# RMSNorm over 16,384 rows on one core: the first store moved ahead of the second tile's load, a coarser first load, and the work split anew over three engines

## The chip, the core and the metric

The kernel runs on one core of a Trainium2 chip. The metric is the device time of one execution in microseconds (us). Before the change, eight runs gave a median of 162.51 us (162.01 to 163.07).

## The reference

The input `x` is 16 x 1024 x 512 in float32, that is 16,384 rows of 512 numbers, 33.55 MB; the output is as large. Each row is divided by its root mean square and multiplied by a vector `gamma` of 512 numbers:

```python
eps = 1e-5
rms = np.sqrt(np.mean(x ** 2, axis=-1, keepdims=True) + eps)
return (x / rms * gamma).astype(np.float32)
```

## The kernel before

**Tiles.** The rows are cut into four tiles. A tile puts R = 32 consecutive rows on each of the 128 partitions, so "a row" below always means one row on every partition: 128 x 512 float32, 262 KB. There are three buffers in on-chip memory (`slot0` to `slot2`), each of one tile; the fourth tile reuses `slot0`. The scaled result overwrites its input in the slot and is stored from there.

**Groups.** A tile is worked on in four groups of G = 8 rows. `row_stats` (from line 65) gives the reciprocal root mean squares of a group, `apply` (line 88) scales its rows, and `transfers` (line 102) asks for the loads and stores that belong after it. The loop at the end of the program takes the statistics of the next group ahead of scaling the present one.

**Engines.** In groups of even number ScalarE squares one row at a time and adds it up in the same operation (line 78; each is followed by a small read of the accumulator). In groups of odd number ScalarE squares four rows into PSUM (line 72) and VectorE adds them up (line 73). ScalarE takes the root (line 84), VectorE the reciprocal (line 85). VectorE alone scales: one operation per row multiplies it by its scalar and by `gamma_b`, a copy of gamma on all partitions (line 90). GpSimd does nothing but set constants. TensorE runs one matrix product, which spreads gamma over the partitions (line 57).

**Queues.** All large transfers are issued by SyncE, loads at line 42 and stores at line 45, in program order: an issue that waits for a semaphore holds every later one. SyncE issues, and the 16 DMA engines move the data. The order is: tile 0 in pieces of 8, 8 and 16 rows, the whole of tile 1, then row 0's store, half of tile 2's load, row 1's store, a quarter of tile 2's load, row 2's store, the last quarter, the rest of tile 0's stores, and so on. A store waits for the scaling of the rows that it takes. A load into `slot0` for tile 3 waits for tile 0's stores.

**Order on the engines.** Before the change, a scheduler chooses the order of each engine's instructions within what the dependences allow.

Of the kernel before, what the change touches and what calls it, by code (L numbers as in the profile page):

```python
# [1 line left out]

# [4 lines left out]


@with_exitstack
def kernel(  # L10
    ctx: ExitStack,
    tc: tile.TileContext,
    x: bass.AP,
    gamma: bass.AP,
    out: bass.AP,
):
    nc = tc.nc
    P = nc.NUM_PARTITIONS
    eps = 1e-5
    fp32 = mybir.dt.float32  # L20
    AF = mybir.ActivationFunctionType
    OP = mybir.AluOpType

    xf = x.flatten_outer_dims()
    of = out.flatten_outer_dims()
    N, D = xf.shape
    R = 32
    G = 8
    H = 4
    assert N == 4 * P * R  # L30

    xv = xf.rearrange("(t p r) d -> t p r d", p=P, r=R)
    ov = of.rearrange("(t p r) d -> t p r d", p=P, r=R)

    const = ctx.enter_context(tc.tile_pool(name="const", bufs=1))
    stats = ctx.enter_context(tc.tile_pool(name="stats", bufs=4))
    psum = ctx.enter_context(tc.tile_pool(name="psum", bufs=2, space=bass.MemoryType.PSUM))

    slots = [const.tile([P, R, D], fp32, name=f"slot{i}") for i in range(3)]

    def load(t, slot, r0, r1):
        nc.sync.dma_start(out=slots[slot][:, r0:r1], in_=xv[t][:, r0:r1])

    def store(t, slot, r0, r1):
        nc.sync.dma_start(out=ov[t][:, r0:r1], in_=slots[slot][:, r0:r1])

    load(0, 0, 0, 8)
    load(0, 0, 8, 16)
    load(0, 0, 16, 32)
    load(1, 1, 0, 32)  # L50

    gamma_row = const.tile([1, D], fp32)
    nc.scalar.dma_start(out=gamma_row, in_=gamma.unsqueeze(0))
    ones_col = const.tile([1, P], fp32)
    nc.vector.memset(ones_col, 1.0)  # L55
    gamma_psum = psum.tile([P, H, D], fp32, name="sq")
    nc.tensor.matmul(gamma_psum[:, 0], ones_col, gamma_row, start=True, stop=True)  # L57
    gamma_b = const.tile([P, D], fp32)
    nc.vector.tensor_copy(out=gamma_b, in_=gamma_psum[:, 0])  # L59

    eps_t = const.tile([P, 1], fp32)
    nc.vector.memset(eps_t, eps)  # L62
    sq_scratch = const.tile([P, D], fp32)

    def row_stats(slot, g):
        ss = stats.tile([P, G], fp32, name="ss")
        rms = stats.tile([P, G], fp32, name="rms")
        rstd = stats.tile([P, G], fp32, name="rstd")
        if (g // G) % 2:
            for h in range(0, G, H):  # L70
                sq = psum.tile([P, H, D], fp32, name="sq")
                nc.scalar.activation(out=sq, in_=slots[slot][:, g + h : g + h + H, :], func=AF.Square)  # L72
                nc.vector.tensor_reduce(  # L73
                    out=ss[:, h : h + H], in_=sq, axis=mybir.AxisListType.X, op=OP.add
                )
        else:
            for r in range(G):
                nc.scalar.activation(  # L78
                    out=sq_scratch,
                    in_=slots[slot][:, g + r, :],  # L80
                    func=AF.Square,
                    accum_out=ss[:, r : r + 1],
                )
        nc.scalar.activation(out=rms, in_=ss, func=AF.Sqrt, bias=eps_t, scale=1.0 / D)  # L84
        nc.vector.reciprocal(out=rstd, in_=rms)  # L85
        return rstd

    def apply(slot, g, rstd):
        for r in range(G):
            nc.vector.scalar_tensor_tensor(  # L90
                out=slots[slot][:, g + r, :],
                in0=slots[slot][:, g + r, :],
                scalar=rstd[:, r : r + 1],
                in1=gamma_b,
                op0=OP.mult,
                op1=OP.mult,
            )

    groups = [(t, g) for t in range(4) for g in range(0, R, G)]
    slot_of = [0, 1, 2, 0]  # L100

    def transfers(t, g):
        if (t, g) == (0, 0):
            store(0, 0, 0, 1)
            load(2, 2, 0, 16)
            store(0, 0, 1, 2)
            load(2, 2, 16, 24)
            store(0, 0, 2, 3)
            load(2, 2, 24, 32)
        elif (t, g) == (0, 24):  # L110
            store(0, 0, 3, 32)
        elif (t, g) == (1, 8):
            store(1, 1, 0, 16)
            load(3, 0, 0, 16)
            load(3, 0, 16, 32)
        elif (t, g) == (1, 24):
            store(1, 1, 16, 32)
        elif (t, g) == (2, 24):
            store(2, 2, 0, 32)
        elif (t, g) == (3, 8):  # L120
            store(3, 0, 0, 16)
        elif (t, g) == (3, 24):
            store(3, 0, 16, 32)

    ahead = row_stats(0, 0)
    for k, (t, g) in enumerate(groups):
        rstd = ahead
        if k + 1 < len(groups):
            tn, gn = groups[k + 1]
            ahead = row_stats(slot_of[tn], gn)  # L130
        apply(slot_of[t], g, rstd)
        transfers(t, g)


# [1 line left out]
_INS = ['x', 'gamma']  # L136
_OUTS = [((16, 1024, 512), 'float32')]


# [23 lines left out]
```

## Time and profile before

The profile is of one execution; the span is from its first to its last instruction on the core.

| | |
|---|---|
| median of 8 runs | 162.51 us |
| the profiled execution's own time | 162.31 us |
| its span | 160.5 us |
| VectorE busy | 122.6 us (76%) |
| ScalarE busy | 80.1 us (50%) |
| GpSimd busy | 0.2 us |
| bytes moved by DMA | 67.13 MB, mean 418 GB/s over the span |

"Busy" is the time in which an engine ran instructions. In a line of the groups of instructions, what follows the name of the operation is out<-in with partitions x elements; after the bar come the busy time in us and the mean duration of one instruction in ns, then the engine's idle time just before them and what ended it. Instructions on one engine overlap a little, so that the step from one start to the next can be shorter than a duration; the chain of waits gives start, length and number of a run of instructions, from which that step is seen.

### The profile page before, as it was taken

To read this page: it belongs to the slowest core of one execution; us is meant where nothing else is said; L and a number is where in the kernel's file an instruction comes from. 1 tells how busy PE (TensorE), PEld (TensorE's weight loads), DVE (VectorE), ACT (ScalarE), POOL (GpSimd) and SP (SyncE) were. 2 spreads that over 40 slices of the span, in tenths; PEclk is the share of its full clock that TensorE was granted. 3 is DMA by queue.
4 is the path that set the end of the run, shared out by engine and by line. 5 is a ranking of instruction groups with operands and counts; after the bars stand their busy time and mean duration, and the time that the engine had idled before them with its cause. 6 is when DMAs were issued, how large, how long until landed. Compare 5 with 4: busy or idle time off the path is not lost.

```text
span 160.5 us, 415 instructions
## 1 busy us (share of the span) xinstructions
PE 2.0 (1%) x2; PEld 0.5 (0%) x2; DVE 122.6 (76%) x163; ACT 80.1 (50%) x162; POOL 0.2 (0%) x4
## 2 busy tenths in 40 slices
PE   4000000000000000000000000000000000000000
PEld 1000000000000000000000000000000000000000
DVE  0102999999995099999999999999999999950000
ACT  3099839910489999969009600796099400000000
POOL 0000000000000000000000000000000000000000
DMA  6999999969799999998799999999999799899993
GB/s 196 445 421 498 400 425 490 523 261 523 327 427 389 452 429 504 474 459 385 340 474 433 400 441 465 400 408 490 400 514 457 343 506 425 367 392 465 449 392 139
DMA packets 2596, 67.13 MB, mean 418 GB/s; under 512 B 289, under 2 KB 289, under 8 KB 674
## 3 DMA queue, kind: packets, MB, share of 16 engines
q1 hardware_dynamic: 2592, 67.11, 97.7%
q14 instruction: 2, 0.02, 0.0%
q10 hardware_dynamic: 2, 0.00, 0.0%
HBM read 33.56 MB, written 33.55 MB: 418 GB/s over the span
## 4 chain that ended last, share of the span: by engine, by line
DVE 69%; ACT 12%; DMA 5%; issue 2%; DVEq 0%
DVE slot L90 51%; DVE ss L73 17%; ACT sq_scratch L78 7%; DMA slot<-in_x_dram 5%; ACT sq L72 4%; DVE rstd L85 1%; ACT rms L84 0%; DVEq L158 0%
## 5 line engine op out<-in xcount | busy, mean ns | idle before, releaser
L90 DVE SCALAR_TENSOR_TENSOR slot<-slot,rstd,gamma_b 128x512 f32<-128x512 f32 x128 | 85.7, 740 | 0.1
L78 ACT ACTIVATE sq_scratch<-slot 128x512 f32<-128x512 f32 x64 | 40.0, 625 | 16.1 <-DMA slot<-in_x_dram 14.8
L73 DVE TENSOR_REDUCE ss<-sq 128x4 f32<-128x2048 f32 x16 | 36.0, 2276 | 10.3 <-ACT sq L72 10.2
L72 ACT ACTIVATE sq<-slot 128x2048 f32<-128x2048 f32 x16 | 29.8, 1861 | 8.3 <-DVE ss L73 8.3
L84 ACT ACTIVATE rms<-ss,eps_t 128x8 f32<-128x8 f32 x16 | 4.6, 298 | 26.6 <-DVE ss L73 26.4
L78 ACT ACTIVATION_READ_ACCUMULATOR sq_scratch<-slot 128x1 f32 x64 | 11.9, 186 | 0.0
L85 DVE RECIPROCAL rstd<-rms 128x8 f32<-128x8 f32 x16 | 3.1, 194 | 5.7 <-ACT rms L84 5.7
L59 DVE COPY gamma_b<-sq 128x512 f32<-128x512 f32 x1 | 0.7, 691 | 3.2 <-PE sq L57 3.2
L57 PE MATMUL sq<-gamma_row,ones_col 1*128 1x512 f32 x2 | 2.0, 1122 | 2.1 <-DMA gamma_row<-in_gamma_dram 2.1
L78 ACT ACT_TABLE_LOAD x1 | 1.3, 1283 | 1.3 <-PEq L147 1.3
L84 ACT ACT_TABLE_LOAD x1 | 1.3, 1283 | 0.0
L55 DVE MEMSET ones_col<- 1x128 f32 x1 | 0.2, 165 | 0.8 <-PEq L147 0.8
L57 PEld LDWEIGHTS sq<-gamma_row,ones_col 1*128 1x128 f32 x2 | 0.5, 306 | 2.1 <-issue 2.1
L147 POOL MEMSET const-bfloat16-1.0<- 128x1 bf16 x1 | 0.1, 101 | 0.0
L147 POOL MEMSET const-uint8-127<- 128x1 uint8 x1 | 0.1, 101 | 0.0
L147 POOL MEMSET const-float32-0.0<- 128x1 f32 x1 | 0.1, 98 | 0.2 <-issue 0.2
L147 POOL MEMSET const-float32-1.0<- 128x1 f32 x1 | 0.1, 98 | 0.0
L62 DVE MEMSET eps_t<- 128x1 f32 x1 | 0.1, 59 | 0.0
## 6 DMA issues: line engine op xcount, KB each, us to landing
slot<-in_x_dram SPq DMA_DIRECT2D x4, 4096.0 KB, 24.9
out_dram<-slot SPq DMA_DIRECT2D x4, 4096.0 KB, 22.4
slot<-in_x_dram SPq DMA_DIRECT2D x4, 2048.0 KB, 11.8
out_dram<-slot SPq DMA_DIRECT2D x1, 7424.0 KB, 35.6
out_dram<-slot SPq DMA_DIRECT2D x3, 256.0 KB, 31.8
gamma_row<-in_gamma_dram ACTq DMA_DIRECT2D x1, 2.0 KB
slot<-in_x_dram SPq DMA_DIRECT2D x1, 40.1
out_dram<-slot SPq DMA_DIRECT2D x1
```

What stands on the lines that cost most here:

```text
L55: nc.vector.memset(ones_col, 1.0)
L57: nc.tensor.matmul(gamma_psum[:, 0], ones_col, gamma_row, start=True, stop=True)
L59: nc.vector.tensor_copy(out=gamma_b, in_=gamma_psum[:, 0])
L62: nc.vector.memset(eps_t, eps)
L72: nc.scalar.activation(out=sq, in_=slots[slot][:, g + h : g + h + H, :], func=AF.Square)
L73: nc.vector.tensor_reduce(out=ss[:, h : h + H], in_=sq, axis=mybir.AxisListType.X, op=OP.add)
L78: nc.scalar.activation(out=sq_scratch, in_=slots[slot][:, g + r, :], func=AF.Square, accum_out=ss[:, r : r + 1],)
L84: nc.scalar.activation(out=rms, in_=ss, func=AF.Sqrt, bias=eps_t, scale=1.0 / D)
L85: nc.vector.reciprocal(out=rstd, in_=rms)
L90: nc.vector.scalar_tensor_tensor(out=slots[slot][:, g + r, :], in0=slots[slot][:, g + r, :], scalar=rstd[:, r : r + 1], in1=gamma_b, op0=O ...
L147: nc = _bacc.Bacc("TRN2", target_bir_lowering=False, num_devices=1)
```

## The change

**Transfers.** Tile 0 is loaded in two pieces, of 8 and 24 rows. Tile 1's load is moved: it is now asked for in `transfers`, behind the store of row 0. Tile 2 is loaded in two halves, with row 1's store between them; row 2 no longer has a store of its own. Tile 0's other rows go out in two stores (14 and 16 rows), asked for after its last group, and the loads of tile 3 stand directly behind them. Tile 1 goes out in one store where it went in two.

**Groups.** The groups are written out: 8, 12 and 12 rows in tile 0, 16 and 16 in the others.

**Statistics.** ScalarE squares 4, 5 or 7 rows at a time, into PSUM and into on-chip memory in turn, with one buffer of each; VectorE adds them all up.

**Scaling.** The last 3 to 7 rows of each group (48 of 128 in all) are scaled by GpSimd in two operations, once by the scalars and once by gamma, each over all these rows. VectorE scales the other 80 rows, with gamma read from PSUM.

**Order.** The scheduler is switched off (`manual_schedule`): every engine runs its instructions in the order of the code. In the code, the sums of the next group stand ahead of the scaling of the present one, and the next group's root and reciprocal stand behind the present group's third row. One instruction on VectorE aligns its code, and some constants are now set by GpSimd.

```diff
+    ctx.enter_context(tc.manual_schedule())
+    nc.vector.addr_align(128, offset=0, max_nops=0)
...
     load(0, 0, 0, 8)
-    load(0, 0, 8, 16)
-    load(0, 0, 16, 32)
-    load(1, 1, 0, 32)
+    load(0, 0, 8, 32)
...
+    groups = [
+        (0, 0, 8, (4, 4), 3),
+        (0, 8, 12, (7, 5), 5),
+        (0, 20, 12, (7, 5), 5),
+        (1, 0, 16, (7, 5, 4), 7),
+        (1, 16, 16, (7, 5, 4), 7),
+        (2, 0, 16, (7, 5, 4), 6),
+        (2, 16, 16, (7, 5, 4), 6),
+        (3, 0, 16, (7, 5, 4), 6),
+        (3, 16, 16, (7, 5, 4), 3),
+    ]
+    slot_of = [0, 1, 2, 0]
+
+    def sum_squares(t, g, n, pieces, share):
+        ss = stats.tile([P, 16], fp32, name="ss")
+        r = 0
+        for k, m in enumerate(pieces):
+            if k % 2:
+                sq = const.tile([P, 5, D], fp32, name="sq_sbuf")
+            else:
+                sq = psum.tile([P, 7, D], fp32, name="sq_psum")
+            rows = slots[slot_of[t]][:, g + r : g + r + m, :]
+            nc.scalar.activation(out=sq[:, :m], in_=rows, func=AF.Square)
+            nc.vector.tensor_reduce(
+                out=ss[:, r : r + m], in_=sq[:, :m], axis=mybir.AxisListType.X, op=OP.add
+            )
+            r += m
+        return ss
+
+    def inverse_rms(ss, n):
+        rms = stats.tile([P, 16], fp32, name="rms")
+        rstd = stats.tile([P, 16, 1], fp32, name="rstd")
+        nc.scalar.activation(out=rms[:, :n], in_=ss[:, :n], func=AF.Sqrt, bias=eps_t, scale=1.0 / D)
+        nc.vector.reciprocal(out=rstd[:, :n, 0], in_=rms[:, :n])
         return rstd
 
+    def scale_by_pool(rstd, t, g, n, pieces, share):
+        part = slots[slot_of[t]][:, g + n - share : g + n, :]
+        by_row = rstd[:, n - share : n].to_broadcast([P, share, D])
+        nc.gpsimd.tensor_tensor(out=part, in0=part, in1=by_row, op=OP.mult)
+        nc.gpsimd.tensor_tensor(out=part, in0=part, in1=gamma_b.to_broadcast([P, share, D]), op=OP.mult)
 
+    def scale_row(rstd, t, g, r):
+        x = slots[slot_of[t]][:, g + r, :]
+        nc.vector.scalar_tensor_tensor(
+            out=x, in0=x, scalar=rstd[:, r], in1=gamma_psum, op0=OP.mult, op1=OP.mult
+        )
 
     def transfers(t, g):
         if (t, g) == (0, 0):
             store(0, 0, 0, 1)
+            load(1, 1, 0, 32)
             load(2, 2, 0, 16)
             store(0, 0, 1, 2)
-            load(2, 2, 16, 24)
-            store(0, 0, 2, 3)
-            load(2, 2, 24, 32)
-        elif (t, g) == (0, 24):
-            store(0, 0, 3, 32)
-        elif (t, g) == (1, 8):
-            store(1, 1, 0, 16)
+            load(2, 2, 16, 32)
+        elif (t, g) == (0, 20):
+            store(0, 0, 2, 16)
+            store(0, 0, 16, 32)
             load(3, 0, 0, 16)
             load(3, 0, 16, 32)
-        elif (t, g) == (1, 24):
-            store(1, 1, 16, 32)
-        elif (t, g) == (2, 24):
+        elif (t, g) == (1, 16):
+            store(1, 1, 0, 32)
+        elif (t, g) == (2, 16):
             store(2, 2, 0, 32)
-        elif (t, g) == (3, 8):
+        elif (t, g) == (3, 0):
             store(3, 0, 0, 16)
-        elif (t, g) == (3, 24):
+        elif (t, g) == (3, 16):
             store(3, 0, 16, 32)
 
-    ahead = row_stats(0, 0)
-    for k, (t, g) in enumerate(groups):
-        rstd = ahead
-        if k + 1 < len(groups):
-            tn, gn = groups[k + 1]
-            ahead = row_stats(slot_of[tn], gn)
-        apply(slot_of[t], g, rstd)
+    rstd = inverse_rms(sum_squares(*groups[0]), groups[0][2])
+    for k, group in enumerate(groups):
+        t, g, n, pieces, share = group
+        scale_by_pool(rstd, *group)
+        following = groups[k + 1 :][:1]
+        for nxt in following:
+            ss = sum_squares(*nxt)
+        for r in range(n - share):
+            scale_row(rstd, t, g, r)
+            if r == 2:
+                for nxt in following:
+                    rstd_next = inverse_rms(ss, nxt[2])
+        rstd = rstd_next
         transfers(t, g)
```

## The prediction

> **What bounds the kernel now.** I read the page's head, queues and groups first, then busy time by stretches, the timeline of the start, the waits of SyncE's queue and the chain of waits.
>
> ```profile
> span 160.5 us, 415 instructions
> ...
> q1 hardware_dynamic: 2592, 67.11, 97.7%
> ...
> L90 DVE SCALAR_TENSOR_TENSOR slot<-slot,rstd,gamma_b 128x512 f32<-128x512 f32 x128 | 85.7, 740 | 0.1
> L78 ACT ACTIVATE sq_scratch<-slot 128x512 f32<-128x512 f32 x64 | 40.0, 625 | 16.1 <-DMA slot<-in_x_dram 14.8
> L73 DVE TENSOR_REDUCE ss<-sq 128x4 f32<-128x2048 f32 x16 | 36.0, 2276 | 10.3 <-ACT sq L72 10.2
> L72 ACT ACTIVATE sq<-slot 128x2048 f32<-128x2048 f32 x16 | 29.8, 1861 | 8.3 <-DVE ss L73 8.3
> ```
>
> SyncE's queue, q1, takes 97.7% of the 16 DMA engines' span. VectorE's groups fill only 122 us. In the stretches the last column is GB/s, the one before it the DMA share:
>
> ```profile
> 0.00:4.00 4.00, 1.86 (x2) 0.50 (x2) 0.17 (x2) 1.28 (x1) 0.20 (x4) 1.00 0.61 197
> 4.00:20.00 16.00, 0.19 (x1) 0.00 (x0) 5.44 (x5) 10.98 (x21) 0.00 (x0) 1.00 1.03 442
> ...
> 60.00:80.00 20.00, 0.00 (x0) 0.00 (x0) 20.00 (x32) 14.48 (x37) 0.00 (x0) 1.00 1.02 436
> ...
> 140.00:156.00 16.00, 0.00 (x0) 0.00 (x0) 2.68 (x5) 0.00 (x0) 0.00 (x0) 1.00 1.01 438
> 156.00:160.50 4.50, 0.00 (x0) 0.00 (x0) 0.00 (x0) 0.00 (x0) 0.00 (x0) 1.00 0.31 131
> ```
>
> The rate is 442 GB/s in pure loading (4 to 20 us), 436 in the middle, 438 in pure storing at the end. The first slice's 0.8 MB at that rate puts the first byte at 2.2 us, the last slice the last byte near 157.4. So 67.1 MB flow without a break at 432 GB/s: one row (262 KB) per 0.607 us, 256 rows in 155.4 us, and 2.9 us remain behind the last byte. The kernel is at the floor of its transfers, and the change removes no byte. It can gain almost nothing; what counts is whether the transfers still never pause.
>
> ```profile
> 0.73 1.89 SPq L42 DMA_DIRECT2D slot<-in_x_dram  x4
> ...
> 8.05 0.63 ACT L78 ACTIVATE sq_scratch<-slot 128x512 f32<-128x512 f32 x1 [5.51 <-DMA slot<-in_x_dram]
> ...
> 19.94 0.75 DVE L90 SCALAR_TENSOR_TENSOR slot<-slot,rstd,gamma_b 128x512 f32<-128x512 f32 x1
> ...
> 20.72 0.35 SPq L45 DMA_DIRECT2D out_dram<-slot  x1
> ...
> 22.67 0.63 ACT L78 ACTIVATE sq_scratch<-slot 128x512 f32<-128x512 f32 x1 [2.53 <-DMA slot<-in_x_dram]
> ```
>
> Four loads are asked for at once, at 0.73 us; the first byte comes 1.47 us later. Rows 0 to 8 are through at 2.2 + 8 x 0.607 = 7.1 and usable at 8.05: 1.0 us from last byte to use. Rows 16 to 32 are through at 21.6 and usable at 22.67. Then tile 1 is already queued. SyncE waits for VectorE for 102.5 us in all (below), yet behind a full queue, so this costs nothing today.
>
> ```profile
> SPq L45 <- DVE slot L90: 102.5, 5, 27.8
> ```
>
> The chain gives steps (start, length, count):
>
> ```profile
> 13.30 1.77 ACT sq L72
> ...
> 20.81 9.90 DVE slot L90 x15
> ...
> 96.95 4.40 DVE ss L73 x2
> ```
>
> A scaling steps at 0.66 us, a four-row sum at 2.20, a four-row square at 1.77. For other sizes I split a step into streaming and a fixed part. Prices: one element a cycle at 0.96 GHz on VectorE (the Trainium skill, "VectorE: DVE Perf Modes", Specifications and the 1x mode), 0.833 ns an element on ScalarE ("ScalarE: Activation LUTs", the step-by-step section). They make 2.13 of the 2.20 us and 1.71 of the 1.77, so about 0.07 is fixed on each. Estimates: sums of 7 and 5 rows 3.80 and 2.74 us, squares 3.06 and 2.20.
>
> **What the Trainium skill says.** "DMA: Bandwidth & Descriptors", Specifications, puts the fabric ceiling at 435 GB/s; the trace's 432 agrees, and is above the 358 that the same table gives as a limit per core. "GPSIMD Engine Reference", section 3.1 (elementwise cycle accounting), gives a two-input tensor_tensor 2.6 cycles an element at 1.2 GHz, 2.17 ns (4497 ns for 2048 measured there); this trace has no such operation. "SBUF — State Buffer", Who interferes with whom: a VectorE operation with at most one SBUF input doesn't contend with GpSimd. That is the case for the new scaling, whose gamma is in PSUM; no run here shows it yet. "VectorE: DVE Perf Modes", the section on the TRN2 errata, gives a fixed 120 cycles for a PSUM source against 58 for SBUF, 62 more (0.065 us); the trace's PSUM sums carry only 0.07 us in all, which speaks against adding it.
>
> **The change part by part.** Written as an account of clock times, from these steps.
>
> *Start.* The 8-row load and its landing stay at 8.05. ScalarE squares 4 and 4, VectorE sums both by about 14.4, then table load 1.28, root 0.3 and reciprocal: scalars at about 16. So far earlier than before. But VectorE's next instructions, in the code's order, are the sums of rows 8 to 20, and the first scaling stands behind them. These rows are in the 24-row load, which is through only at 21.6 and usable at 22.65. Square 7: 25.7. Sum 7: 29.6. Sum 5: 32.3. Scaling of row 0: 33.0. Only now does the store of row 0 go out, and behind it on SyncE, in program order, stand tile 1's load, both halves of tile 2 and row 1's store. First byte 1.47 us later: 34.5. The transfers pause from 21.6 to 34.5: **12.9 us**. Nothing hides that; at a full rate elsewhere it is not won back. The unknown is the 1.47 (seen for a load at launch): 0.6 to 2.0 as ends, so 12.0 to 13.4.
>
> *Middle.* From 34.5 the queue holds row 0, tile 1 (54.6, usable 55.6), half of tile 2 (64.3), row 1 (64.9), the other half (74.6). Tile 0's 14 rows are scaled by 47 on VectorE and need GpSimd's share by 46, so that store follows at once (83.1). VectorE then waits for tile 1: square 58.7, three sums (8.74) 67.5, seven scalings and a reciprocal (4.74) 72.2: tile 0's last store is asked for in time (92.8). Tile 3's two loads wait for these stores to land, at 84.1 and 93.8, each with a transfer still ahead of it: no pause (112.2). Tile 1: a group takes 8.74 + 9 x 0.66 + 0.12 = 14.8 us, so 87.0 and 101.8, ahead of 112.2; its store runs to 131.6.
>
> *Tile 2's store.* Groups now take 8.74 + 10 x 0.66 + 0.12 = 15.5: 117.2 and 132.7. It is one store of the whole tile, so it goes out at 132.7, first byte 134.2, while the queue ran dry at 131.6: **2.6 us**. Then tile 2 to 153.6, tile 3's halves (ready at 148.1 and 156.7, wanted at 153.6 and 163.3) to 173.1, and 2.9 behind: 176.0.
>
> *VectorE.* It sums all 128 rows instead of 64 and scales 80 instead of 128: 80 x 0.66 + 128 x 0.533 + 24 x 0.07 = 123 us in steps, against 128 x 0.66 + 16 x 2.20 = 120 now. So GpSimd's help is spent on the sums that ScalarE gives up. Reading gamma from PSUM is the unknown: 0.60 (the sums' fixed 0.07 on 0.533) to 0.73 (0.66 plus the page's 62 cycles); I keep 0.66. The 45 scalings between tile 1's landing and 132.7 move this pause by 45 x 0.06 = 2.7 us down (to none) or 45 x 0.07 = 3.2 up.
>
> *GpSimd.* At 2.17 ns, 7 rows twice cost 2 x 3584 x 2.17 = 15.6 us, 6 rows 13.4. Starting with tile 1's first scalars at 69.6 it runs 85.2, 100.8, 114.3, 127.7, five under VectorE's 132.7. Its first use, five rows and three rows before, is due at 47. Ends: if cheaper, nothing changes; at 2.6 it would finish tile 2 at 139.3.
>
> *ScalarE.* 128 rows x 0.427 plus fixed parts, about 60 us instead of 80, always ahead of VectorE after each landing: worth nothing. The accumulator reads (11.9 us) go, off the path. The aligning instruction and the moved constants: nothing, under the first load's 8 us. Fewer stores save SyncE issues of 0.4 us, hidden under the queue.
>
> *Sum.* 160.5 + 12.9 + 2.6 = 176.0 of span; 1.8 us lie around the span (162.31 - 160.5) and the median is 0.2 above the profiled execution: **178.0 us**.
>
> **The rivals.**
> - *Only the first pause.* VectorE steps at 0.60 with gamma in PSUM, or the restart is quick; tile 2's store is in time. 160.5 + 12.9 + 2.0 = 175.4. For it: the PSUM sums' small fixed part. Against: the scaling has two inputs and a scalar.
> - *GpSimd becomes the bound.* Its price is from a page alone, and both operations have a repeated operand. It decides from (132.7 - 69.6) / 58.1 x 2.17 = 2.36 ns. At 2.6: tile 2 asked for at 139.3, a pause of 9.2 instead of 2.6, so 184.6. Against: the shares of 6 and 7 rows fit VectorE's groups at 2.17.
> - *Not slower: the gate opens early.* Place: VectorE's first scaling. If the first store were asked for by 20.1 (21.6 - 1.47), as it would be were that scaling not held behind the sums of rows 8 to 20 (scalars stand at 16), the first pause of 12.9 goes. Tile 2's store would then still come late by about 4 us at a step of 0.66, and in time only at 0.58: 160.5 of span again, 162.5. Against: the manual order, and that both must hold. A faster transfer afterwards can't do it: winning back 15.5 of 155.4 us needs 480 GB/s, and the best of the 20-us stretches (100 to 120 us) shows 455.
>
> **How the numbers follow.** Two pauses as worked: 0.62, with a range of 176 to 181 from the step (0.62 to 0.73) and the restart. First pause alone, 175.4: 0.14. GpSimd bound, 182 to 190: 0.20. Gate early, 162.5: 0.04. The range of 174 to 185 takes the first two and the near half of the third. About 0.3% (0.5 us) is what a measurement here can tell from no change: faster 0.02, same 0.02 (the two halves of the last case), slower 0.96.
>
> **What would show it.** In the profile after: a DMA share near nothing from about 22 to 34 us; the first store's issue at about 33 and not 20.7; SyncE's longest wait at its start, on VectorE's scaling; ScalarE's square of tile 1 waiting on its load until about 55.6; a second pause near 132, of 0 to 6 us; GpSimd about 107 us busy (49,152 elements x 2.17). It is wrong if the first store goes out before 21 us, if the rate after the gap is above 450 GB/s, or if GpSimd's step is over 2.36 ns an element.

## The result and the profile after

The changed kernel takes 176.07 us in the median of 11 runs (175.83 to 177.17); the kernel before took 162.51 in the 32 runs beside it. The ratio is 1.0845, with a 95% interval of 1.0829 to 1.0861: 13.6 us slower. The forecast was 178.0 with a range of 174 to 185. The profiled execution took 176.68 us, its span is 175.0.

The head, the queue of the transfers and the costliest groups of the page after (DVE is VectorE, ACT is ScalarE, POOL is GpSimd; SPq is the queue of SyncE, which issues the transfers):

```profile
span 175.0 us, 275 instructions
...
q1 hardware_dynamic: 2160, 67.11, 90.2%
...
L103 POOL TENSOR_TENSOR slot<-slot,rstd 128x3072 f32<-128x3072 f32 (+3 forms) x9 | 42.6, 4738 | 52.7 <-DVE rstd L97 52.7
L87 DVE TENSOR_REDUCE ss<-sq_psum 128x7 f32<-128x3584 f32 (+1 forms) x15 | 47.0, 3135 | 31.9 <-ACT sq_psum L86 31.8
L86 ACT ACTIVATE sq_psum<-slot 128x3584 f32<-128x3584 f32 (+1 forms) x15 | 38.3, 2556 | 45.7 <-DMA slot<-in_x_dram 23.0
L104 POOL TENSOR_TENSOR slot<-slot,gamma_b 128x3072 f32<-128x3072 f32 (+3 forms) x9 | 53.5, 5946 | 0.7
L108 DVE SCALAR_TENSOR_TENSOR slot<-slot,rstd,gamma_psum 128x512 f32<-128x512 f32 x80 | 53.3, 729 | 0.0
```

The same bytes now fill 90.2% of the engines' span, where it was 97.7%. In us that is 157.9 of 175.0 against 156.8 of 160.5: the transfers work as long as before, and what was added is time in which they stand still, 17.1 instead of 3.7. VectorE is busy for 123.6 us (122.6 before), so it wasn't relieved. The busy time by stretches shows where the transfers stand still. Behind the length of a stretch stand the busy us of TensorE, of its weight loads, of VectorE, ScalarE and GpSimd, then the clock, the DMA share and GB/s:

```profile
20.00:24.00 4.00, 0.00 (x0) 0.00 (x0) 0.00 (x0) 0.68 (x1) 3.42 (x1) 1.00 0.32 135
24.00:28.00 4.00, 0.00 (x0) 0.00 (x0) 1.48 (x1) 4.00 (x2) 0.00 (x0) 1.00 0.00 0
28.00:32.00 4.00, 0.00 (x0) 0.00 (x0) 4.00 (x2) 0.74 (x1) 0.00 (x0) 1.00 0.00 0
32.00:36.00 4.00, 0.00 (x0) 0.00 (x0) 4.00 (x7) 2.83 (x2) 0.68 (x1) 1.00 0.97 328
```

The timeline of that time tells why:

```profile
8.80 1.88 ACT L86 ACTIVATE sq_psum<-slot 128x2048 f32<-128x2048 f32 x1 [3.71 <-DMA slot<-in_x_dram]
...
16.91 0.20 DVE L97 RECIPROCAL rstd<-rms 128x8 f32<-128x8 f32 x1 [1.71 <-ACT rms L96]
...
23.32 3.16 ACT L86 ACTIVATE sq_psum<-slot 128x3584 f32<-128x3584 f32 x1 [6.45 <-DMA slot<-in_x_dram]
...
26.52 3.89 DVE L87 TENSOR_REDUCE ss<-sq_psum 128x7 f32<-128x3584 f32 x1 [9.41 <-ACT sq_psum L86]
30.32 2.81 DVE L87 TENSOR_REDUCE ss<-sq_sbuf 128x5 f32<-128x2560 f32 x1
33.05 2.05 DVE L108 SCALAR_TENSOR_TENSOR slot<-slot,rstd,gamma_psum 128x512 f32<-128x512 f32 x3
...
33.81 0.35 SPq L46 DMA_DIRECT2D out_dram<-slot  x1
34.21 0.92 SPq L43 DMA_DIRECT2D slot<-in_x_dram  x2
...
56.34 3.16 ACT L86 ACTIVATE sq_psum<-slot 128x3584 f32<-128x3584 f32 x1 [12.84 <-DMA slot<-in_x_dram]
```

The first scalars are ready at 17.1. VectorE then stands for 9.41 us before the sum of rows 8 to 14, because the 24-row load is usable only at 23.32. The first scaling follows the sums at 33.05, the store of row 0 goes out at 33.81, and the load of tile 1 directly after it. ScalarE can use that load only at 56.34, after a wait of 12.84 us.

### The profile page after: what moved, and what is told of

Same layout as the page of the kernel before. It is cut to its first block, busy times and chain, and to the rows that moved or that the text cites. A ratio compares the mean times of both kernels' runs of the same rounds, so it can differ in the third digit from the quotient of the medians.

```text
span 175.0 us, 275 instructions
## 1 busy us (share of the span) xinstructions
PE 2.0 (1%) x2; PEld 0.5 (0%) x2; DVE 123.6 (71%) x113; ACT 63.6 (36%) x36; POOL 96.5 (55%) x24
## 3 DMA queue, kind: packets, MB, share of 16 engines
q1 hardware_dynamic: 2160, 67.11, 90.2%
## 4 chain that ended last, share of the span: by engine, by line
DVE 56%; DMA 25%; ACT 4%; issue 3%; SPq 0%; DVEq 0%
DVE ss L87 31%; DMA slot<-in_x_dram 25%; DVE slot L108 24%; ACT sq_psum L86 4%; DVE rstd L97 1%; DVEq L172 0%; SPq L43 0%; SPq L46 0%
## 5 line engine op out<-in xcount | busy, mean ns | idle before, releaser
L103 POOL TENSOR_TENSOR slot<-slot,rstd 128x3072 f32<-128x3072 f32 (+3 forms) x9 | 42.6, 4738 | 52.7 <-DVE rstd L97 52.7
L87 DVE TENSOR_REDUCE ss<-sq_psum 128x7 f32<-128x3584 f32 (+1 forms) x15 | 47.0, 3135 | 31.9 <-ACT sq_psum L86 31.8
L86 ACT ACTIVATE sq_psum<-slot 128x3584 f32<-128x3584 f32 (+1 forms) x15 | 38.3, 2556 | 45.7 <-DMA slot<-in_x_dram 23.0
L104 POOL TENSOR_TENSOR slot<-slot,gamma_b 128x3072 f32<-128x3072 f32 (+3 forms) x9 | 53.5, 5946 | 0.7
L108 DVE SCALAR_TENSOR_TENSOR slot<-slot,rstd,gamma_psum 128x512 f32<-128x512 f32 x80 | 53.3, 729 | 0.0
L87 DVE TENSOR_REDUCE ss<-sq_sbuf 128x5 f32<-128x2560 f32 (+1 forms) x9 | 24.7, 2747 | 0.0
L86 ACT ACTIVATE sq_sbuf<-slot 128x2560 f32<-128x2560 f32 (+1 forms) x9 | 20.5, 2273 | 0.0
L96 ACT ACTIVATE rms<-ss,eps_t 128x16 f32<-128x16 f32 (+2 forms) x9 | 2.8, 306 | 27.1 <-DVE ss L87 27.1
L97 DVE RECIPROCAL rstd<-rms 128x16 f32<-128x16 f32 (+2 forms) x9 | 2.1, 233 | 1.7 <-ACT rms L96 1.7
L56 PE MATMUL gamma_psum<-gamma_row,ones_col 1*128 1x512 f32 x2 | 2.0, 1122 | 2.4 <-DMA gamma_row<-in_gamma_dram 2.4
## 6 DMA issues: line engine op xcount, KB each, us to landing
slot<-in_x_dram SPq DMA_DIRECT2D x1, 6144.0 KB, 22.1
```

Source lines behind the costliest of these rows:

```text
L56: nc.tensor.matmul(gamma_psum, ones_col, gamma_row, start=True, stop=True)
L86: nc.scalar.activation(out=sq[:, :m], in_=rows, func=AF.Square)
L87: nc.vector.tensor_reduce(out=ss[:, r : r + m], in_=sq[:, :m], axis=mybir.AxisListType.X, op=OP.add)
L96: nc.scalar.activation(out=rms[:, :n], in_=ss[:, :n], func=AF.Sqrt, bias=eps_t, scale=1.0 / D)
L97: nc.vector.reciprocal(out=rstd[:, :n, 0], in_=rms[:, :n])
L103: nc.gpsimd.tensor_tensor(out=part, in0=part, in1=by_row, op=OP.mult)
```

## The experiments

Every kernel was timed beside the kernel before on its chip; ratios are to that.

**1. Tile 1's load at launch.**

```diff
     load(0, 0, 8, 32)
+    load(1, 1, 0, 32)
...
             store(0, 0, 0, 1)
-            load(1, 1, 0, 32)
```

> The changed kernel with tile 1's load asked for at launch again, before row 0's store; all else as changed. Theory (the held load opens the first pause): the transfers no longer pause at 21 us, tile 1 is usable near 42 and VectorE runs on without a wait after tile 0, so tile 2's store is asked for near 121.5, while the queue is dry at about 118.5: a second pause of about 4 instead of 1 to 2.6 us. Time 165.5 to 167. Rival (the loss is spread over the slower flow of VectorE and GpSimd, and the pause at the start only shifts it): it stays above 172.

Measured: 164.19 us, 1.0109 (1.0089 to 1.0130), span 162.6. This one line is worth 11.9 of the 13.6 us. Row 0's store still goes out late (33.74), but now behind a full queue. The rival, which expected more than 172, falls. The time is 1.3 us under the theory's lower end, so the second pause costs less than worked out, although it is there: the store of tile 2 was asked for at 121.45, and the records have little from 119 to 122:

```profile
119.00:122.00 3.00, 0.00 (x0) 0.00 (x0) 3.00 (x5) 1.38 (x1) 3.00 (x1) 1.00 0.05 22
```

**2. The same, and tile 2 stored in halves.**

```diff
+        elif (t, g) == (2, 0):
+            store(2, 2, 0, 16)
         elif (t, g) == (2, 16):
-            store(2, 2, 0, 32)
+            store(2, 2, 16, 32)
```

> As the one before, and tile 2 is stored in two halves, the first asked for after its first group. Theory: both pauses are gone, the transfers run without a break, 162.5 (162 to 163.3), no different from the kernel before. Rival (VectorE and GpSimd together are too slow for the transfers): 165 or more, with pauses before later stores.

Measured: 163.81 us, 1.0092 (1.0068 to 1.0115), span 162.0. Neither fits: the kernel isn't back at 162.5, and not at 165. The second pause is worth at most 0.4 us here (the intervals of experiments 1 and 2 overlap), and about 1.3 us stay. The end of the record shows something of them, here the stretches of this kernel:

```profile
158.00:159.00 1.00, 0.00 (x0) 0.00 (x0) 0.00 (x0) 0.00 (x0) 0.00 (x0) 1.00 0.08 33
159.00:160.00 1.00, 0.00 (x0) 0.00 (x0) 0.00 (x0) 0.00 (x0) 0.00 (x0) 1.00 0.08 33
```

33 GB/s for 1 us is 33 KB, one packet of one of the 16 engines, which takes 1.2 us and is booked at its start. The packets of the trace, taken one by one, agree: fifteen engines end between 158.05 and 158.31 us, and one, which still has two packets to move, ends at 160.59. In the kernel before, no data packet starts after 158 (0 GB/s from 158 to 159 us), and the last engine ends at 159.13, 0.6 after the next.

**3. The halves alone, with tile 1's load still held.** The second edit of experiment 2 on the changed kernel.

> The changed kernel with tile 2 stored in two halves, and the load of tile 1 still held. Theory (a second pause stands before tile 2's store): its 1.2 to 2.6 us go, 173.5 to 174.9. Rival (the low rate near 132 us in the records is a matter of when packets are written down and no pause): 176.1, no change.

Measured: 175.51 us, 1.0808 (1.0785 to 1.0831), against 1.0845 (1.0829 to 1.0861): some 0.6 us, between the two, and the intervals just overlap, so the times alone don't decide. In the trace of the changed kernel the second pause is seen here:

```profile
130.00:132.00 2.00, 0.00 (x0) 0.00 (x0) 2.00 (x4) 2.00 (x1) 2.00 (x1) 1.00 1.21 524
132.00:134.00 2.00, 0.00 (x0) 0.00 (x0) 2.00 (x3) 0.23 (x1) 2.00 (x1) 1.00 0.08 33
134.00:136.00 2.00, 0.00 (x0) 0.00 (x0) 2.00 (x1) 0.00 (x0) 1.92 (x2) 1.00 1.23 524
```

A packet of 64 KB takes 2.4 us and is booked at its start, so the slice from 132 to 134 isn't 2 us of standstill. The one packet in it is again of one engine alone. Packet by packet, fifteen engines end tile 1's store between 132.97 and 133.52 and begin tile 2's at 134.15 to 134.27; the sixteenth ends at 135.04 and goes on at once.

**4. Tile 0 loaded in 8, 12 and 12 rows.**

```diff
-    load(0, 0, 8, 32)
+    load(0, 0, 8, 20)
+    load(0, 0, 20, 32)
```

> The changed kernel with tile 0 loaded in 8, 12 and 12 rows, in the sizes of its groups, and tile 1's load still held. Theory (the first scaling waits for the sums of rows 8 to 20, these for the whole 24-row piece): rows 8 to 20 are usable near 16, squares from 17, sums until 26.6, row 0's store at 27.3 instead of 33.8, so the first pause is 6.5 us shorter; VectorE's later steps shift by the same, so the second stays: 169.0 to 170.2. Rival (only the place of the load matters, not the size of the pieces): 175.5 to 176.5.

Measured: 169.82 us, 1.0470 (1.0440 to 1.0501), as the theory has it. The timeline of this kernel has the squares early and row 0's store with them:

```profile
16.61 3.14 ACT L87 ACTIVATE sq_psum<-slot 128x3584 f32<-128x3584 f32 x1
...
27.09 0.35 SPq L46 DMA_DIRECT2D out_dram<-slot  x1
```

The store is 6.7 us earlier and the kernel 6.2 us faster. So the coarse load makes about half of the first pause; the rest is the squares and sums that still stand ahead of the scaling.

**5. The first group's scalings ahead of the next group's sums.** The load is held and the 24-row piece stays; only the order on VectorE differs.

```diff
+        for r in range(n - share if k == 0 else 0):
+            scale_row(rstd, t, g, r)
         for nxt in following:
             ss = sum_squares(*nxt)
+            if k == 0:
+                rstd_next = inverse_rms(ss, nxt[2])
-        for r in range(n - share):
+        for r in range(n - share if k else 0):
```

> The changed kernel with one edit in the order of the code: in the first group, the scalings stand ahead of the sums of the next group. The load of tile 1 is still held behind row 0's store, the 24-row piece stays. Theory (the order on VectorE opens the pause): row 0's store goes out near 18, no pause at 21; then as with tile 1 loaded at launch, tile 2's store is about 4 us late: 165.5 to 167. Rival (the place of the load or the 24-row piece is what counts): above 172.

Measured: 164.73 us, 1.0143 (1.0123 to 1.0162). Row 0's store goes out at 17.71, in the timeline of SyncE's queue:

```profile
17.71 0.35 SPq L46 DMA_DIRECT2D out_dram<-slot  x1
18.11 0.90 SPq L43 DMA_DIRECT2D slot<-in_x_dram  x2
```

The order alone takes 11.3 us away. Holding the load costs little here (164.73 against 164.19 in experiment 1); what costs is that its gate, the store in front of it, opens late. The time is again a little under the range, as in experiment 1.

**6. The same, and tile 2 in halves.**

> As the one before, and tile 2 is stored in two halves. Theory: no pause is left, 162.0 to 163.2, as the kernel before, since the transfers' 155.4 us and about 5 us at both ends are common to both. Rival (a freer VectorE, which no longer limits, shortens the ends): under 161.5.

Measured: 164.18 us, 1.0100 (1.0082 to 1.0119). Both miss. It equals experiment 2 within the intervals, by another way: with both pauses dealt with, the changed kernel stands at about 1.01.

**7. The kernel before with tile 1's load held.**

```diff
-    load(1, 1, 0, 32)
...
             store(0, 0, 0, 1)
+            load(1, 1, 0, 32)
```

> The kernel before with one edit: tile 1's load is asked for behind row 0's store, as in the change. Here the scheduler puts the first scaling ahead of the later sums and row 0's store goes out at 20.7. Theory (the held load costs only what the store is late by): restart 1 to 1.5 us after 20.7, against the end of tile 0's bytes at 21.3 to 21.6: a pause of 0.2 to 0.9 us, 162.6 to 163.6. Rival (holding the load is costly in itself, whatever VectorE's order): 170 or more.

Measured: 164.95 us, 1.0146 (1.0119 to 1.0173). The store went out at 20.55, as expected, and the rival's 170 is far off, but the loss is 2.5 us where the theory had at most 1. In the trace the engines end apart: the rate falls over the last 2 us (328, 262, 197, 66 GB/s in its last four half-microseconds with packets). By the packets they come apart at the restart: they end tile 0's last load within 0.4 us of each other (21.7 to 22.1), but tile 1's within 2.0 (42.7 to 44.7; 41.3 to 41.8 in the kernel before). So a held load isn't free even when its gate opens before the queue is empty. Why the engines come apart there stays open.

**8. Gamma read from on-chip memory by VectorE.**

```diff
-            out=x, in0=x, scalar=rstd[:, r], in1=gamma_psum, op0=OP.mult, op1=OP.mult
+            out=x, in0=x, scalar=rstd[:, r], in1=gamma_b[:, 0], op0=OP.mult, op1=OP.mult
```

> The changed kernel with VectorE reading gamma from on-chip memory (the copy that GpSimd reads) instead of PSUM: its scaling then has two inputs there. Theory ([...]such an operation and a GpSimd operation that reads there exclude each other): the first pause is as before, since GpSimd is idle when row 0 is scaled; later VectorE's 6 us of scalings in a group can't run beside GpSimd's 12 to 14, a group takes about 20 instead of 15 us, tile 2's store is 15 to 20 us later: 185 to 196, and mean durations rise well above 0.73 us a scaling or above GpSimd's 5.3 and 6.7. Rival (they share without loss): 176.

Measured: 240.75 us, 1.4819 (1.4797 to 1.4841). The mechanism holds, and the price was far too low. The first line is of the changed kernel, the second of this one: minimum, median and maximum of a scaling in ns.

```profile
L108 DVE SCALAR_TENSOR_TENSOR slot<-slot,rstd,gamma_psum x80: 646/736/743, 33.1 to 156.4; 128x512 f32<-128x512 f32 x80
```

```profile
L108 DVE SCALAR_TENSOR_TENSOR slot<-slot,rstd,gamma_b x80: 650/741/8209, 32.8 to 225.1; 128x512 f32<-128x512 f32 x80
```

And two stretches of this kernel, 16 us of scaling and 9 of sums:

```profile
72.00:88.00 16.00, 0.00 (x0) 0.00 (x0) 16.00 (x6) 3.62 (x2) 14.57 (x2) 1.00 0.75 313
88.00:97.00 9.00, 0.00 (x0) 0.00 (x0) 9.00 (x5) 2.06 (x2) 0.00 (x0) 1.00 0.95 408
```

A scaling that meets a GpSimd operation waits here until that ends, and takes up to 8.2 us; GpSimd's 7-row operation itself hardly grows (6.16 to 6.52 us). I had let GpSimd run beside the sums. But the sums stand behind the blocked scalings in VectorE's order, so nothing overlaps: GpSimd 14.6, then sums 8.8 and the other scalings, about 27 us a group instead of 20.

**9 and 10. Where the last 1.3 us come from: transfers or work?** In experiment 9 the new division of work, with the first rows first, has the old list of transfers (tile 2 in halves). In 10 the kernel before has experiment 2's list. The core of 9, then of 10:

```diff
-    load(0, 0, 8, 32)
+    load(0, 0, 8, 16)
+    load(0, 0, 16, 32)
+    load(1, 1, 0, 32)
...
-            store(0, 0, 2, 16)
-            store(0, 0, 16, 32)
+            store(0, 0, 3, 32)
```

```diff
-    load(0, 0, 8, 16)
-    load(0, 0, 16, 32)
+    load(0, 0, 8, 32)
...
-            store(0, 0, 3, 32)
+            store(0, 0, 2, 16)
+            store(0, 0, 16, 32)
```

> The changed kernel's division of work, with the first group's scalings first, and the transfers of the kernel before (loads of 8, 8 and 16 rows, tile 1's load at launch, three one-row stores among tile 2's load, tile 0's other rows in one store, tile 1 in halves); only tile 2 is stored in halves. Asked: where the 1.3 to 1.7 us come from that stay when both pauses are gone. Theory A (they come with the list of transfers: in coarser pieces one DMA engine of the 16 ends later than the others): gone here, 162.2 to 163.0. Theory B (they come with the work on the engines, GpSimd's reads and writes among them, which disturb the transfers): 163.8 to 164.3.

> The kernel before in its work on the engines, with the transfers of the experiment that had both pauses removed (8 and 24 rows, tile 1's load at launch, tile 2's load in halves, tile 0 stored as 1, 1, 14 and 16 rows, tile 1 whole, tile 2 in halves). Theory A (the list of transfers): 163.6 to 164.3. Theory B (the work on the engines): 162.2 to 163.0.

Measured: 164.25 us, 1.0118 (1.0100 to 1.0136), and 162.14 us, 0.9988 (0.9978 to 0.9997). The loss goes with the new code on the engines and not with the list of transfers. That code is more than the division of work: the order by hand, the aligning instruction and the constants set by GpSimd come with it in every experiment. Experiment 10 is the best kernel seen, by 0.1 to 0.2%, too little to call a gain here. Its end, to be held against that of experiment 2:

```profile
158.00:159.00 1.00, 0.00 (x0) 0.00 (x0) 0.00 (x0) 0.00 (x0) 0.00 (x0) 1.00 0.08 33
159.00:160.00 1.00, 0.00 (x0) 0.00 (x0) 0.00 (x0) 0.00 (x0) 0.00 (x0) 1.00 0.00 0
```

**11 and 12. Is it GpSimd?** Both on experiment 2's kernel. In 11 the multiplication by gamma is left out for GpSimd's 48 rows; in 12 ScalarE scales these rows, without gamma too, and its scalings stand behind the next group's squares.

```diff
-        nc.gpsimd.tensor_tensor(out=part, in0=part, in1=gamma_b.to_broadcast([P, share, D]), op=OP.mult)
```

```diff
-        nc.gpsimd.tensor_tensor(out=part, in0=part, in1=by_row, op=OP.mult)
-        nc.gpsimd.tensor_tensor(out=part, in0=part, in1=gamma_b.to_broadcast([P, share, D]), op=OP.mult)
+        for r in range(n - share, n):
+            row = slots[slot_of[t]][:, g + r, :]
+            nc.scalar.activation(out=row, in_=row, func=AF.Copy, scale=rstd[:, r])
...
-        scale_by_pool(rstd, *group)
...
+        scale_by_pool(rstd, *group)
```

> The experiment with both pauses removed (tile 1's load at launch, tile 2 stored in halves; 1.0092 of the kernel before), with GpSimd's second operation left out: the multiplication by gamma is missing for its 48 rows, and GpSimd is busy 43 instead of 97 us. Theory (GpSimd's work beside the transfers makes one DMA engine late): about half of the 1.3 to 1.7 us go, 162.9 to 163.4. Rival (VectorE's and ScalarE's new work, the squares written to on-chip memory among it, does it): 163.7 to 164.3.

> The same base, with GpSimd's rows scaled by ScalarE row by row behind the next group's squares; the multiplication by gamma is missing for these 48 rows, and GpSimd only sets constants. Theory (GpSimd's work makes one DMA engine late): the whole 1.3 to 1.7 us go, 162.1 to 162.8, and all DMA engines end together. Rival (VectorE's and ScalarE's new work): 163.7 to 164.3, one engine late as before.

Measured: 163.99 us, 1.0111 (1.0081 to 1.0140), and 164.47 us, 1.0130 (1.0103 to 1.0157). My theory of GpSimd falls: without any of its scaling the loss is still there (experiment 12 lies even above the rival's range), and one engine is still late in the stretches of experiment 12:

```profile
158.00:159.00 1.00, 0.00 (x0) 0.00 (x0) 0.00 (x0) 0.00 (x0) 0.00 (x0) 1.00 0.08 33
159.00:160.00 1.00, 0.00 (x0) 0.00 (x0) 0.00 (x0) 0.00 (x0) 0.00 (x0) 1.00 0.08 33
```

**What the traces show of the late engine.** It is late before any engine has touched a row. The first lines of ScalarE say when the first load, of the same eight rows in both, could be used; experiment 10 stands first, 9 second:

```profile
7.92 0.63 ACT L77 ACTIVATE sq_scratch<-slot 128x512 f32<-128x512 f32 x1 [5.36 <-DMA slot<-in_x_dram]
```

```profile
8.59 1.88 ACT L88 ACTIVATE sq_psum<-slot 128x2048 f32<-128x2048 f32 x1 [3.80 <-DMA slot<-in_x_dram]
```

It is 7.88 to 8.05 us in the three kernels with the old work (the one before, 7 and 10) and 8.57 to 8.89 in all eleven with the new. In each of the eleven, an 8 KB packet of the queue that brings instructions (q14 on the page) stands at 3.6 to 3.9 us, and the data packet that starts as it ends takes 1.14 us instead of 0.61. In the eight traces in which the late engine can be followed back from the end of the first load without doubt, this packet is on it. In the old kernels no such packet falls into the first load; they come at 46 to 49 and 60 to 64 us. With it the last engine ends the first load 0.5 to 0.8 us behind the next one, against 0.15 at most in the old kernels. So a fetch of instructions makes the start of the lag. In experiment 2 the lag has grown to 2.3 us by 65 us and then stays. Where the rest comes from, and whether it is VectorE's and ScalarE's new work, wasn't taken apart and stays open.

## Why the prediction was right, and where its sum was off

**The mechanism.** It was as forecast: the held load, the coarse 24-row piece and the order on VectorE together open a pause at the start. Each of the three, undone alone, removes its share: 11.9 us (experiment 1), 6.2 (4) and 11.3 (5). They aren't added up, since any one that puts the load on the queue in time closes the pause.

**The first pause, forecast 12.9 us, measured 11.7 to 11.9** (experiments 3 and 2 differ by the held load alone: 175.51 - 163.81 = 11.7 us; 1 against the changed kernel 11.9). The mis-sized term is the end of tile 0's bytes. The forecast has all 16 engines through at 21.6, from one rate for all. In the trace of the changed kernel fifteen end the 24-row load between 21.66 and 22.04 us and the sixteenth at 22.96. Row 0's first packet starts at 34.66, where 34.5 was forecast, but by two errors that cancel: the store was asked for at 33.81 instead of 33.0, since that load was usable at 23.32 instead of 22.65, and the first packet followed after 0.85 us instead of 1.47 (at launch too it follows after 1.0, at 1.74 us; the 2.2 came from taking the full rate from the first byte on). So fifteen engines stand still for nearly 13 us, as forecast, and the late one for 11.7. What the pause added to the time agrees with the late one.

**The second pause, forecast 2.6 us, measured 0.4 to 0.6** (experiments 2 and 3, neither clear of the intervals). Its place and cause are as forecast: tile 2's store was asked for at 133.31 (forecast 132.7). Its cost is lower, for two reasons. The fifteen engines ran dry at 133.0 to 133.5 instead of 131.6, and so stand still for about 1 us. And the late engine, which ends the kernel, hardly stands still at all. In experiment 1, where the pause is longer, fifteen engines stand still from about 119.5 until 122.3, but the late one ends at 122.03 and so loses only 0.3 us, and after the pause all 16 are in step (they end within 0.2 us of each other, at 161.1 to 161.3). In the changed kernel it loses nothing. This is read from the packets; no run removes the lag to test it.

**A term that was missing: 1.3 to 1.9 us.** The sum took the floor of the transfers as the same for any division of work, and put the aligning instruction and the moved constants at nothing, as being under the first load. Experiments 2, 6 and 9 have no pause that I can see and stand at 1.0092 to 1.0118. That the forecast of 178.0 came within 2 us of 176.07 is in part luck: the pauses were put 3.2 us too high (12.9 + 2.6 against 11.7 + 0.6), and the missing 1.3 made up for part of it. The steps 11.7, 0.6 and 1.3 are differences of the same runs, so that they add up to the 13.6 proves nothing.

**VectorE.** The step with gamma in PSUM stayed at 0.66 us: ten scalings take 6.58 us in the chain of the changed kernel,

```profile
150.59 6.58 DVE slot L108 x10
```

against 6.62 in the kernel before. So the 62 cycles that the Trainium skill ("VectorE: DVE Perf Modes", the section on the TRN2 errata) adds for a PSUM source don't show in the step here, where one of two inputs is in PSUM. Three sums in a row took 8.72 to 8.81 us in the chain (8.74 estimated).

**GpSimd** was busy for 96.5 us where 107 were forecast, and finished tile 2's rows at 125.5, well before VectorE. The rival in which it becomes the bound is out: its step would have had to be 2.36 ns an element, and six rows in both operations (5310 and 6662 ns for 3072 elements each) make 1.95 on average.

**Other rivals.** "Only the first pause" gave 175.4 and comes nearest in its number. The restart was quicker, as it says, but the step wasn't shorter, and tile 2's store wasn't in time for fifteen of the engines; the second pause is there and costs little for another reason. "The gate opens early" is what experiments 5 and 6 build, and their times show what it would have given: 164.7 and 164.2, slower than the 162.5 it was credited with.

## What to carry to other kernels

When transfers fill the whole span, look at what each issue in the queue waits for, and at what stands ahead of that on the engine it waits for: a store used as a gate holds every later load, and its price here was close to the time from the end of the queued bytes to the gate's opening. With the order written by hand, the first instruction that a gate waits for belongs ahead of everything that waits for a later transfer; that alone was worth 11.3 us here. Moving work between engines gained nothing here while the transfers were the floor, and came with a per cent that no busy time explains. When the transfers fill the span, look at the 16 DMA engines one by one: the last of them sets the time.

## What the runs showed of the hardware

- The two GpSimd operations differ: with the scalar repeated along the row it takes 2746 ns for 1536 elements and 6158 for 3584, that is 1.67 ns an element; with the gamma row repeated over the rows 3426 and 7758, 2.12 ns. The Trainium skill ("GPSIMD Engine Reference", section 3.1) gives 2.6 cycles an element for two inputs, 2.17 ns at 1.2 GHz; the second agrees, the first is nearly a quarter under it.
- A VectorE scaling with both inputs in on-chip memory waits for a GpSimd operation that reads there; with one of the inputs in PSUM it doesn't, as the Trainium skill ("SBUF — State Buffer", Who interferes with whom) has it: with gamma in PSUM a scaling took 743 ns at most beside a busy GpSimd, with gamma in on-chip memory up to 8209.
- Of the 16 DMA engines one can end 2.3 us behind the others (experiment 2), and then it sets the time. It came with the new code on the engines and not with the list of transfers, and GpSimd's scaling isn't needed for it.
- A fetch of instructions delays a DMA engine's data: an 8 KB packet of q14 that took 0.31 us made the 16 KB data packet behind it take 1.14 us instead of 0.61, in all eleven kernels with the new code. This starts the lag, at 0.5 to 0.8 us; the cause of the rest is open.
- A pause can put the engines in step again: in experiment 1 they are 2.4 us apart before the second pause and 0.2 at the end.
